# A conformer convolution's finish one attention step earlier, with two of its operations moved to VectorE

## The chip, the cores and the metric

The kernel runs on one core of one Trainium2 chip. The metric is device microseconds of one execution, given as the median of several runs. A core has TensorE (matrix products, written PE in the profile), VectorE (DVE), ScalarE (ACT), GpSimd (POOL) and SyncE (SP), each with its own queue of instructions that it takes in order; here SP issues the weight loads. All five share the on-chip memories: SBUF for tiles, and PSUM, into which TensorE writes and which VectorE and ScalarE read.

## What is computed

A trunk of two layers on 512 positions of width 1024. Each layer is a feed-forward part, a mixing part and a second feed-forward part. The change lies in the mixing part, in the convolution group:

```python
def conv_module(a, g, conv_w, conv_b, conv_norm):
    u = a * jax.nn.sigmoid(g)
    y = lax.conv_general_dilated(u, rhs, ...)      # causal, depthwise, width 31
    y = y + conv_b
    return jax.nn.silu(rms_norm(y, conv_norm))

# mixing part of a layer
a, g, q, k, v = jnp.split(rms_norm(x, mix_norm[l]) @ w_in[l], splits, axis=-1)
conv_out = conv_module(a, g, conv_w[l], conv_b[l], conv_norm[l])
# per head: two softmax maps with a relative-position bias, A1 - lambda * A2, values, RMSNorm
diff_out = diff_attention(q, k, v, rel_bias, lam, lam_init, subln_norm[l])
x = x + jnp.concatenate([conv_out, diff_out], axis=-1) @ w_out[l]
```

## The kernel before

Activations lie with features on the 128 partitions and the 512 positions along the free axis. Every large product is made of three products in a fast 32-bit format: each factor is split into a larger part (a rounded copy) and a lower part (the value minus that copy), and `mm3` adds larger x larger, larger x lower and lower x larger. For weights the larger part `whi` is made by ScalarE (L101) and the lower part `wlo` by VectorE or GpSimd (L102), from a buffer `wraw` that SP loads.

A program that schedules by estimated times places the instructions of each engine; only those wrapped in `keep_in_program_order` keep the written order. So moving one operation can change the order of its neighbours on every engine.

The mixer's stages around the change:

- `conv_in` and `project` make the convolution's inputs, queries and keys; `project_values` the values.
- `conv_taps` computes the 31 taps of four channel tiles `ys[0..3]`. Tile 0 and ten taps of tile 3 are done by ScalarE and GpSimd (L968, L969, result `yp`), the rest by VectorE (L983, result `u`). `conv_square` adds up the squares; with the last tile GpSimd multiplies all four tiles by half the gain (`ghalf`, L955).
- `rows_rstd` transposes the sum of squares on TensorE (L196), reduces it on VectorE (L200, L201) and GpSimd raises it to -1/2 (L189, `rs_y`).
- `attend(n)` runs one attention step; step n is one head of one block of 128 queries, with 512, 384, 256 and 128 keys for steps 0 to 3, 4 to 7, 8 to 11 and 12 to 15. `softmaxes` has TensorE's two scores (L1015), VectorE's pass that adds the bias and finds the minimum (L1019), ScalarE's exponential (L1023), and VectorE's reciprocal, factor and combination of the two maps (L1026, L1028, L1029). Two steps later `keys_first` transposes the map (L1036, copied by ScalarE, L1038), three steps later `values` multiplies it with the values (L1045). With a block's last head, VectorE sums squares (L1056), GpSimd makes the root, VectorE scales (L1060), and `block_out` transposes the block (L1072) and splits it into parts (L1074 ScalarE, L1075 VectorE).
- `conv_finish`, called behind one attention step, spreads the statistic over the positions (`spread`: TensorE L209, ScalarE L213) and for each of the four tiles: GpSimd multiplies by the statistic (L995), ScalarE takes the tanh (L997), VectorE forms the swish (L998), ScalarE makes the larger part (L999, into `ch`), GpSimd the lower part (L1000, into `cl`).
- `next_wo` loads and splits one of four chunks of the output weights for the convolution half; two of these calls stand behind `conv_finish`.
- The output projection (L138, L141, L142 with `ps_out`) first takes the convolution's four feature tiles for all eight output tiles, then the attention's features; VectorE adds each result to x (L1137).

PSUM has two buffers under each of the tags `sc` and `po`, which scores and output products share, two under `mm` for the value products, and one each under `tp` and `y`.

Of the kernel before, what the change touches and what calls it, by code (L numbers as in the profile page):

```python
# [14 lines left out]
AF = mybir.ActivationFunctionType  # L15
ALU = mybir.AluOpType
# [52 lines left out]
def trunk(ctx: ExitStack, tc: tile.TileContext, xt, par, lamv, relb, onehot,  # L69
          gu1, dn1, wag, wqkv, wout, gu2, dn2, out):  # L70
    nc = tc.nc
    V, S, G, T = nc.vector, nc.scalar, nc.gpsimd, nc.tensor
# [9 lines left out]
    def f32(ap):  # L82
        return ap.bitcast(F32)
# [3 lines left out]
    def bank(tag, name):  # L87
        return psum.tile([P, 512], F32, tag=tag, name=name, bufs=BANKS[tag])
# [115 lines left out]
    def spread(rc, tag, pin=False):  # L204


        ps = bank("y", "ps_spread")
        for j in range(NT):
            mm = T.transpose(ps[:, j * P : (j + 1) * P], rc[:, j : j + 1].broadcast_to([P, P]), ident)  # L209
            if pin:  # L210
                tc.keep_in_program_order(mm)
        r = act.tile([P, SEQ], F32, tag=tag, name=tag)
        S.activation(r, ps, AF.Copy)  # L213
        return r
# [585 lines left out]
    nlam, gq, gsub, ghalf = [], [], [], []  # L800
# [35 lines left out]
    def mixer(l, pr, after, turn):  # L836
        with tc.tile_pool(name="mix", bufs=1) as mp, tc.tile_pool(name="mt", bufs=2) as mt:
# [101 lines left out]
            ch, cl = acth, actl  # L939

            ys = [None] * CT
            csum = mp.tile([P, SEQ], F32, tag="csum", name="csum")

            def conv_square(c, y):
                if c == 0:
                    S.activation(csum, y, AF.Square)
                else:
                    sq = mt.tile([P, SEQ], F32, tag="csq", name="csq", bufs=1)
                    S.activation(sq, y, AF.Square)
                    G.tensor_tensor(csum, csum, sq, op=ALU.add)  # L950

                if c == CT - 1:
                    for k in range(CT):
                        tc.keep_in_program_order(
                            G.tensor_scalar(ys[k], ys[k], ghalf[l][:, k : k + 1], None, op0=ALU.mult)  # L955
                        )

            def conv_taps(c, n, then=None):

# [10 lines left out]
                if n == TAPS:  # L970
                    ys[c] = yp
                    conv_square(c, yp)
                    return
# [13 lines left out]
                if n:  # L987
                    V.tensor_tensor(ys[c], y, yp, op=ALU.add)
                conv_square(c, ys[c])

            def conv_finish(rcv):
                rcv = spread(rcv, "rb")
                for c in range(CT):
                    z = ys[c]
                    G.tensor_tensor(z, z, rcv, op=ALU.mult)  # L995
                    th = bank("y", "ps_th")
                    S.activation(th, z, AF.Tanh)  # L997
                    V.scalar_tensor_tensor(z, th, 1.0, z, op0=ALU.add, op1=ALU.mult)  # L998
                    S.activation(ch[:, c, :], z, AF.Copy)  # L999
                    G.tensor_tensor(cl[:, c, :], z, f32(ch[:, c, :]), op=ALU.subtract)  # L1000


# [76 lines left out]
            def attend(n):  # L1079
                if n < len(steps):  # L1080
                    softmaxes(*steps[n])
                if 2 <= n < len(steps) + 2:
                    keys_first(*steps[n - 2])
                if 3 <= n < len(steps) + 3:
                    values(*steps[n - 3])
                if n >= 5 and steps[n - 5][1] == HEADS - 1:
                    block_out(steps[n - 5][0])
# [23 lines left out]
            def next_wo():  # L1111
                wo.append(chunk(wout[l, 0, len(wo)], G, pin=True))
# [4 lines left out]
            next_wo()  # L1117
            for n in range(2, len(steps) + 5):
                attend(n)
                if n == 8:  # L1120
                    conv_finish(rcv)
                    next_wo()
                    next_wo()
# [3 lines left out]
            for half, t in ((0, slice(0, SEQ)), (1, slice(SEQ // 2, SEQ)), (1, slice(0, SEQ // 2))):  # L1127
                if t.stop == SEQ:
                    w = [None] * 4 if half else wo
                for m in range(KT):  # L1130
# [3 lines left out]
                    for kk in range(4):  # L1134
                        k = half * 4 + kk
# [17 lines left out]
    for l in range(DEPTH):  # L1153
        nxt = {}

        def then(l2, gain):
            def after(m):
                if m == 0:
                    nxt["p"] = Prep(l2, gain)
                nxt["p"].tile(m)  # L1160
            return after

        def last(m):
            nc.sync.dma_start(out[m], x[:, m, :])

        turn = ffn(pr, gu1[l], dn1[l], then(l, "mix_norm"), 2, *((lead, aside) if l == 0 else ()))
        mixer(l, nxt["p"], then(l, "ffn2_norm"), turn)
        ffn(nxt["p"], gu2[l], dn2[l], then(l + 1, "ffn1_norm") if l + 1 < DEPTH else last, 0)
        pr = nxt["p"]
# [74 lines left out]
```

## Time and profile before

| | us |
|---|---|
| median of 3 runs | 1775.17 (1773.5 to 1775.44) |
| the profiled execution | 1775.55 |
| its span, first to last instruction | 1773.8 |
| TensorE busy | 1762.1 |
| VectorE busy | 1420.0 |
| ScalarE busy | 995.8 |
| GpSimd busy | 999.0 |

A row of a timeline has the start in us from the span's start, the duration in us (for merged rows that of all xN together), engine, line, operation, the tile written and the tiles read, their shapes, the count, and in brackets the idle time ahead of it with the engine and line that ended it. On VectorE, ScalarE and GpSimd a row's duration runs a little past the start of the next one, so the price of an operation in a full queue is the distance of the starts. A row of a group view has the count, then total busy us and mean ns of one. A row for a tile or a line has the durations in ns as least, median and largest, and the first and the last start. In the windows the columns are the window, its length, busy us of PE, PE's weight loads, DVE, ACT and POOL with the number of instructions, the granted TensorE clock as a share of full speed, the share of the DMA engines' time and GB/s.

### The profile page before, as it was taken

What the parts mean: (1) busy time and instruction counts of PE and PEld (TensorE: products, weight loads), DVE (VectorE), ACT (ScalarE), POOL (GpSimd) and SP (SyncE); (2) the same over time, 40 slices, a digit from 0 to 9 for tenths busy, and PEclk for the clock granted to TensorE, in tenths of its full rate; (3) what the DMA queues carried; (4) which work ended last, traced back from release to release, by engine and by line L of the source; (5) the groups of instructions that cost most, each with busy time, mean ns of one, the idle gap of its engine ahead of it and who ended that gap; (6) DMA issues with size and microseconds to landing.
All of it is one profiled execution on the core that took longest, in us unless ns stands there. A gap on an engine that the chain in (4) does not pass through costs nothing.

```text
span 1773.8 us, 30569 instructions
## 1 busy us (share of the span) xinstructions
PE 1762.1 (99%) x11869; PEld 1624.1 (92%) x11869; DVE 1420.0 (80%) x2021; ACT 995.8 (56%) x1591; POOL 999.0 (56%) x665
## 2 busy tenths in 40 slices
PE   9999999999999999999999999999999999999999
PEld 7899999988788899999988999999887988999998
DVE  6988888868857878888778888877788488788885
ACT  6456566645845456556534665665558354565663
POOL 3176766379863156656304666653898432567661
PEclk9999999999999999999999999999999999999999
DMA  6233333433122233333332333334230232333332
GB/s 225 92 117 96 107 108 105 124 106 96 36 84 84 83 97 107 107 101 120 101 109 71 108 98 106 108 102 148 72 119 25 72 108 72 108 96 108 108 105 75
DMA packets 74227, 177.89 MB, mean 100 GB/s; under 512 B 8952, under 2 KB 30727, under 8 KB 74081
## 3 DMA queue, kind: packets, MB, share of 16 engines
q1 hardware_dynamic: 72480, 174.10, 31.3%
q8 instruction: 93, 1.52, 0.4%
q0 software_dynamic: 1312, 1.67, 0.3%
q14 instruction: 54, 0.43, 0.1%
q10 hardware_dynamic: 288, 0.16, 0.0%
HBM read 173.79 MB, written 3.42 MB: 100 GB/s over the span
## 4 chain that ended last, share of the span: by engine, by line
PE 89%; DVE 6%; issue 2%; POOL 2%; ACT 1%; DMA 0%; ACTq 0%; SPq 0%; DVEq 0%
PE ps_pair L378 49%; PE ps_pair L142 5%; PE ps_pair L141 5%; PE ps_pair L138 5%; DVE wlo L368 2%; PE ps_d L138 2%; PE ps_d L142 2%; PE ps_d L141 2%; PE ps_sc L1015 2%; PE ps_d L378 2%; PE ps_pair L891 2%; PE ps_pair L893 2%; PE ps_pair L892 2%; PE ps_out L138 1%; PE ps_out L141 1%
## 5 line engine op out<-in xcount | busy, mean ns | idle before, releaser
L368 DVE TENSOR_TENSOR wlo<-wraw,whi 128x1024 fp32r<-128x1024 f32 (+2 forms) x400 | 525.4, 1314 | 149.7 <-ACT whi L364 149.0
L364 ACT ACTIVATE whi<-wraw 128x1024 fp32r<-128x1024 f32 (+2 forms) x400 | 378.6, 948 | 312.1 <-PE ps_pair L378 144.5
L355 POOL TENSOR_TENSOR wraw<-wraw 128x512 f32<-128x512 f32 (+1 forms) x100 | 132.1, 1321 | 519.7 <-DVE wlo L368 316.2
L378 PE MATMUL ps_pair<-actl,whi 128*128 128x256 f32 x1088 | 307.9, 283 | 0.0
L378 PE MATMUL ps_pair<-acth,wlo 128*128 128x256 f32 x1088 | 307.9, 283 | 0.0
L378 PE MATMUL ps_pair<-acth,whi 128*128 128x256 f32 x1088 | 307.9, 283 | 0.0
L378 PE MATMUL ps_pair<-th,whi 128*128 128x256 f32 x816 | 232.5, 285 | 2.4 <-ACT keep L430 1.5
L378 PE MATMUL ps_pair<-tl,whi 128*128 128x256 f32 x816 | 230.9, 283 | 0.0
L378 PE MATMUL ps_pair<-th,wlo 128*128 128x256 f32 x816 | 230.8, 283 | 0.0
L378 PEld LDWEIGHTS ps_pair<-acth,whi 128*128 128x128 f32 x1088 | 208.9, 192 | 0.2
L378 PEld LDWEIGHTS ps_pair<-actl,whi 128*128 128x128 f32 x1088 | 208.9, 192 | 0.2
L378 PEld LDWEIGHTS ps_pair<-acth,wlo 128*128 128x128 f32 x1088 | 208.9, 192 | 0.0
L101 ACT ACTIVATE whi<-wraw 128x1024 fp32r<-128x1024 f32 (+3 forms) x124 | 122.9, 1000 | 147.9 <-PE ps_pair L141 79.7
L358 POOL TENSOR_TENSOR wraw<-wraw 128x512 f32<-128x512 f32 (+1 forms) x100 | 177.4, 1774 | 7.9
L141 PE MATMUL ps_pair<-actl,whi 128*128 128x512 f32 x448 | 174.7, 391 | 0.3
L138 PE MATMUL ps_pair<-acth,whi 128*128 128x512 f32 x448 | 173.9, 393 | 0.4 <-ACT whi L101 0.4
L142 PE MATMUL ps_pair<-acth,wlo 128*128 128x512 f32 x448 | 173.8, 390 | 0.0
L357 POOL TENSOR_TENSOR wraw<-wraw 128x512 f32<-128x512 f32 (+1 forms) x100 | 169.0, 1690 | 7.8
L356 POOL TENSOR_TENSOR wraw<-wraw 128x512 f32<-128x512 f32 (+1 forms) x100 | 166.9, 1669 | 7.6
L378 PEld LDWEIGHTS ps_pair<-th,whi 128*128 128x128 f32 x816 | 156.5, 192 | 5.3 <-ACT keep L430 4.9
L378 PEld LDWEIGHTS ps_pair<-tl,whi 128*128 128x128 f32 x816 | 156.5, 192 | 0.0
L378 PEld LDWEIGHTS ps_pair<-th,wlo 128*128 128x128 f32 x816 | 156.5, 192 | 0.0
(205 smaller groups left out, 4461.3 us busy)
## 6 DMA issues: line engine op xcount, KB each, us to landing
wraw<-in_gu SPq DMA_DIRECT2D x172, 512.0 KB, 3.5
wraw<-in_wqkv SPq DMA_DIRECT2D x24, 512.0 KB, 3.6
wraw<-in_wag SPq DMA_DIRECT2D x16, 512.0 KB, 3.6
wraw<-in_wout SPq DMA_DIRECT2D x16, 512.0 KB, 3.5
wraw<-in_dn SPq DMA_DIRECT2D x60, 128.0 KB, 3.0
wraw<-in_dn SPq DMA_DIRECT2D x20, 384.0 KB, 3.3
wraw<-in_dn SPq DMA_DIRECT2D x28, 256.0 KB, 3.3
wraw<-in_dn SPq DMA_DIRECT2D x20, 320.0 KB, 3.3
```

What stands on the lines that cost most here:

```text
L101: S.activation(hi, raw, AF.Copy)
L138: first = T.matmul(ps, wh, xh, start=start, stop=False)
L141: T.matmul(ps, wh, xl, start=False, stop=False)
L142: T.matmul(ps, wl, xh, start=False, stop=stop)
L355: G.tensor_tensor(d, g1, u1, op=ALU.add)
L356: G.tensor_tensor(u1, u1, u2, op=ALU.add)
L357: G.tensor_tensor(m0, u1, g1, op=ALU.add)
L358: G.tensor_tensor(m1, m0, g2, op=ALU.add)
L364: pinned(S.activation(hi[:, : self.cols[k]], self.raw[k][:, : self.cols[k]], AF.Copy), pin)
L368: pinned(V.tensor_tensor(out=lo[:, :c], in0=self.raw[k][:, :c], in1=f32(hi[:, :c]), op=ALU.subtract), pin)
L378: mm = T.matmul(ps, l, r, start=first and i == n == 0, stop=False, skip_group_check=True)
L891: T.matmul(ps[n], xh[:, t], wh, start=k == 0, stop=False)
```

## The change

Three edits, in both layers:

```diff
                 if c == CT - 1:
                     for k in range(CT):
-                        tc.keep_in_program_order(
-                            G.tensor_scalar(ys[k], ys[k], ghalf[l][:, k : k + 1], None, op0=ALU.mult)
-                        )
+                        V.tensor_scalar(ys[k], ys[k], ghalf[l][:, k : k + 1], None, op0=ALU.mult)
...
                     V.scalar_tensor_tensor(z, th, 1.0, z, op0=ALU.add, op1=ALU.mult)
-                    S.activation(ch[:, c, :], z, AF.Copy)
+                    V.tensor_scalar(ch[:, c, :], z, 1.0, None, op0=ALU.mult)
                     G.tensor_tensor(cl[:, c, :], z, f32(ch[:, c, :]), op=ALU.subtract)
...
             for n in range(2, len(steps) + 5):
                 attend(n)
-                if n == 8:
+                if n == 7:
                     conv_finish(rcv)
                     next_wo()
                     next_wo()
```

The four multiplications by half the gain go from GpSimd to VectorE and are no longer held in the written order; the four copies that make the larger parts go from ScalarE to VectorE; and `conv_finish` with its two `next_wo` calls is written behind step 7 where it was behind step 8. Line numbers of the changed kernel are two lower from L957 on.

## The prediction

> **What bounds the kernel now.** I read the page's engine shares first, then the windows across the first layer's mixer, then the timelines of TensorE, VectorE and GpSimd where TensorE has gaps.
>
> ```profile
> PE 1762.1 (99%) x11869; PEld 1624.1 (92%) x11869; DVE 1420.0 (80%) x2021; ACT 995.8 (56%) x1591; POOL 999.0 (56%) x665
> ```
>
> TensorE sets the time nearly everywhere, so the change can act only where TensorE waits. In the mixer of the first layer that is one place:
>
> ```profile
> 465.00:470.00 5.00, 5.00 (x22) 3.32 (x21) 2.18 (x5) 5.00 (x8) 3.97 (x4) 1.00 0.00 0
> ...
> 485.00:490.00 5.00, 5.00 (x42) 4.78 (x40) 4.31 (x21) 3.95 (x16) 3.92 (x5) 1.00 0.32 94
> 490.00:495.00 5.00, 3.20 (x20) 2.25 (x19) 4.88 (x19) 5.00 (x18) 4.67 (x6) 1.00 0.03 11
> ```
>
> ```profile
> 1370.00:1375.00 5.00, 3.20 (x20) 2.24 (x19) 4.88 (x19) 5.00 (x19) 4.68 (x6) 1.00 0.06 25
> 1375.00:1380.00 5.00, 5.00 (x25) 4.60 (x24) 3.70 (x13) 4.37 (x16) 3.29 (x4) 0.66 0.00 0
> ```
>
> The columns are window, then busy time of TensorE, its weight loads, VectorE, ScalarE and GpSimd, then the granted clock. From 490 to 495 TensorE has holes, while VectorE (4.88) and ScalarE (5.00) are full. The second layer repeats this 880 us later, and just behind its holes the granted clock is 0.66 over 5 us, so up to 5 x 0.34 = 1.7 us more are lost there. TensorE's own rows:
>
> ```profile
> 489.84 0.39 PE L1015 MATMUL ps_sc<-kt,qz 128*128 128x128 f32 x2
> 490.43 0.70 PE L1015 MATMUL ps_sc<-kt,qz 128*128 128x256 f32 x2 [0.20 <-DVE e L1029]
> 490.97 0.38 PE L1036 MATMUL ps_at<-ident,e 128*128 128x128 f32 x2
> 491.19 0.60 PE L1072 MATMUL ps_o<-ident,ov 128*128 128x128 f32 x4
> 492.05 0.49 PE L1015 MATMUL ps_sc<-kt,qz 128*128 128x128 f32 x2 [0.26 <-DVE mn L1019]
> 493.04 0.49 PE L1015 MATMUL ps_sc<-kt,qz 128*128 128x128 f32 x2 [0.50 <-DVE e L1029]
> 493.36 0.38 PE L1036 MATMUL ps_at<-ident,e 128*128 128x128 f32 x2
> 494.57 1.16 PE L1045 MATMUL ps_o<-vv,at 128*128 128x128 f32 x8 [0.83 <-DVE actl L1075]
> 495.49 0.48 PE L138 MATMUL ps_out<-acth,whi 128*128 128x512 f32 x1
> ```
>
> A 128-column piece costs 0.11 us (eight in 495.49 - 494.57 = 0.92), a 256-column score 0.22. From 489.84 to 495.49 are 5.65 us with 2x0.11 + 2x0.22 + 2x0.11 + 4x0.11 + 2x0.11 + 2x0.11 + 2x0.11 + 0.92 = 2.90 of work: **2.75 us of holes in each layer**, all released by VectorE. At 495.49 the first output product (L138) arrives and fills TensorE from there. So the question is what stands ahead of that product, and how fast VectorE gets through it:
>
> ```profile
> 481.43 0.23 DVE L201 TENSOR_SCALAR rowv<-rowv 128x4 f32<-128x4 f32 x1
> ...
> 486.04 0.62 DVE L1029 SCALAR_TENSOR_TENSOR e<-ps_sc,c,e 128x384 f32<-128x384 f32 x1
> ...
> 490.30 0.68 DVE L1060 TENSOR_TENSOR ov<-ps_o,rs_y 128x512 f32<-128x512 f32 x1
> 490.89 0.15 DVE L1026 RECIPROCAL r<-sums 128x1 f32<-128x1 f32 x1
> 491.17 0.43 DVE L1019 CUSTOM_DVE_ANT_0 ps_sc<-ps_sc,bias 128x256 f32<-128x256 f32 x1
> ...
> 491.52 0.27 DVE L1028 TENSOR_SCALAR c<-r,nlam,sums 128x1 f32<-128x1 f32 x1
> 491.70 0.28 DVE L1019 CUSTOM_DVE_ANT_0 e<-ps_sc,bias 128x128 f32<-128x128 f32 x1
> ...
> 491.91 0.68 DVE L1056 TENSOR_REDUCE so<-sq 128x4 f32<-128x512 f32 x1
> 492.51 0.47 DVE L1029 SCALAR_TENSOR_TENSOR e<-ps_sc,c,e 128x256 f32<-128x256 f32 x1
> 492.90 0.15 DVE L1026 RECIPROCAL r<-sums 128x1 f32<-128x1 f32 x1
> 492.99 0.69 DVE L998 SCALAR_TENSOR_TENSOR yp<-ps_th,yp 128x512 f32<-128x512 f32 x1
> 493.60 0.27 DVE L1028 TENSOR_SCALAR c<-r,nlam,sums 128x1 f32<-128x1 f32 x1
> 493.78 0.74 DVE L1075 SCALAR_TENSOR_TENSOR actl<-ps_o,gsub,acth 128x512 fp32r<-128x512 f32 x1
> 494.44 0.29 DVE L1019 CUSTOM_DVE_ANT_0 ps_sc<-ps_sc,bias 128x128 f32<-128x128 f32 x1
> ```
>
> Consecutive starts give VectorE's prices: L1060 0.59, L1019 0.35 (256 wide) and 0.21 (128), L1056 0.60, L1029 0.39 (256), L998 0.61, L1075 0.66, L1026 about 0.1, L1028 about 0.2. The row at 492.51 is step 10's combination; the row at 486.04 is step 7's.
>
> **The change part by part.**
>
> *Factor off GpSimd.* The rows below show the four L955 (1.57 us each) just ahead of the conv statistic's rs_y (484.02), whose input was done at 481.66 (481.43 + 0.23). Without them rs_y runs about 2.4 us earlier. What stands behind it on GpSimd stays (a 2.36 us wlo, the block's so and rs_y), so L995 starts near 481.7 + 1.0 + 2.4 + 0.2 + 1.0 = 486.3, about 3 us ahead of 489.63.
>
> ```profile
> 479.42 4.64 POOL L955 TENSOR_SCALAR u<-u,ghalf 128x512 f32<-128x512 f32 x3
> 484.02 1.03 POOL L189 TENSOR_TENSOR rs_y<-rowv,mhalf 128x4 f32<-128x4 f32 x1
> 485.03 2.36 POOL L102 TENSOR_TENSOR wlo<-wraw,whi 128x1024 fp32r<-128x1024 f32 x1
> ...
> 489.63 1.27 POOL L995 TENSOR_TENSOR yp<-yp,rb 128x512 f32<-128x512 f32 x1 [1.00 <-ACT rb L213]
> 490.86 3.20 POOL L995 TENSOR_TENSOR u<-u,rb 128x512 f32<-128x512 f32 x3
> ...
> 503.36 7.09 POOL L102 TENSOR_TENSOR wlo<-wraw,whi 128x1024 fp32r<-128x1024 f32 x3
> ```
>
> *Factor and larger parts onto VectorE.* Eight one-input SBUF operations of 128x512 per layer. The nearest rows:
>
> ```profile
> L201 DVE TENSOR_SCALAR rowv<-rowv 128x4 f32<-128x4 f32 x8 | 1.5, 182 | 0.1
> L99 DVE TENSOR_SCALAR whi<-wraw 128x128 fp32r<-128x128 f32 x1 | 0.2, 227 | 3.2 <-DMA wraw<-in_gu 3.2
> ```
>
> ```profile
> L325 DVE TENSOR_TENSOR actl<-hn,acth x32: 676/686/1786, 60.8 to 1490.2; 128x512 fp32r<-128x512 f32 x32
> ```
>
> ```profile
> L999 ACT ACTIVATE acth<-u x6: 622/632/652, 496.0 to 1382.2; 128x512 fp32r<-128x512 f32 x6
> ```
>
> From 4 to 128 elements the price grows by 45 ns, 0.36 ns an element; 384 more make 0.227 + 0.14 = 0.37, my lower end and, being the same kind of operation, the value I take rounded to 0.4. The upper end is the largest L325 of the same size, 1.8. Three of the four factors stand ahead of step 2's passes, where the window 465 to 470 has VectorE idle for 2.8 us: they cost nothing, and were that cover gone, 1.2 us. The fourth and the four parts fall into the full stretch. ScalarE gets 4 x 0.63 = 2.5 us back, but it does not release TensorE here.
>
> *Finish one step earlier.* The built order tells what that moves. TensorE's queue is in order, and the first output product stands no earlier in it: the same scores, plus two more value products of step 10 (4 x 0.11) and one more block transpose (4 x 0.11), so 0.88 us more work stands ahead, and the product now waits for step 10's combination and its copy. On VectorE the finish used to stand behind that combination (L998 first at 492.99, after 492.51). Now three L998, two parts, one L1075 and a second L1060 stand ahead of it. The two wout loads keep their place in SP's queue, and their GpSimd halves (503.36) still follow the last lower part, early enough for a product some 30 matmuls behind the first. The new order also adds a wait: ScalarE's first tanh (L997) now stands ahead of step 9's second exponential, and VectorE's factor for step 9 queues behind that; L995 ends near 486.3 + 1.3 = 487.6, about when ScalarE gets there, so I cost it at nothing, and at what L995 is late otherwise.
>
> *The sum.* From step 7's combination to the start of step 10's: before, 492.51 - 486.04 = 6.47 us, waits included. After, VectorE's queue holds between them: the combination itself 0.57, six passes of 256 (2.1), two of 128 (0.42), two combinations (0.8), reciprocals and factors (1.15), two L1060 (1.2), one L1056 (0.6), one L1075 (0.66), three L998 (1.83), two parts (0.8): 10.1 us. Step 7's combination itself starts some 0.3 earlier, at 485.7 (two passes of 256 have moved behind it, the fourth factor ahead of it). Step 10's ends at 485.7 + 10.1 + 0.4 = 496.2; transposes 0.22, ScalarE's copy
>
> ```profile
> 495.56 0.42 ACT L1038 ACTIVATE at<-ps_at 128x256 f32<-128x256 f32 x1
> ```
>
> of 0.42, value products 0.44 and about 0.1 for each of four hand-overs make 1.5: the first product starts near 497.7. By before's pace with 0.88 us more work it would be 495.49 + 0.88 = 496.4. That is +1.3 us a layer. In its fullest neighbourhood VectorE still idled 0.69 us in 485 to 490; I add half a microsecond for such hand-overs, which my sum lacks: **+1.8 us a layer, +3.6 in all**, with a low end of +1.0 a layer (no hand-overs, copies at 0.37 in part hidden) and a high end of +3.2 (each of the two parts ahead at about 1.1, halfway to the stretched row). Behind that product I find nothing new late: the parts for its later steps are done before TensorE reaches them. The profiled execution is 1775.55 us (span 1773.8 and 1.75 around it), 0.4 over the median of the three runs, so 1775.55 + 3.6 = **1779.2**.
>
> **The rivals.**
>
> *A. The holes close.* If the finish, 3 us earlier, let TensorE fill its holes, 2 x 2.75 = 5.5 us would go, and with them the clock loss of up to 1.7: 1768.4 to 1770. For it: VectorE releases every hole, and GpSimd and ScalarE get lighter. Against: no product moved ahead in TensorE's queue, and VectorE, which is full, got more. It decides only if step 10's combination comes before about 494.
>
> *B. Slower by less than can be told.* The low end, or the clock loss of the second layer falling away: 1775.55 + 3.6 - 1.7 = 1777.5. For it: the clock fell in one layer only, although both have the same holes, so whether it falls is close to a toss. [...]
>
> *C. VectorE and GpSimd shut each other out.* L325 takes 0.68 at best and 1.79 at worst. In the finish GpSimd is nearly always busy (4.67 of 5), with operations of 1.1 to 2.4 us; if each part waited for the rest of one, some 0.6 to 1.1, two of them ahead would add 1.2 to 2.2 a layer: 1779.2 + 3 = 1782. [...] No row here has a one-input VectorE operation of this size under a busy GpSimd.
>
> **How the numbers follow.** Forecast 0.46, A 0.10, B 0.30, C 0.14. About 0.2%, 3.6 us, is what can be told from no change. Slower by more than that: forecast and C, 0.60; within: B, 0.30; faster: A, 0.10. The range for 8 in 10 leaves out A and the far end of C: 1775.5 to 1783.0.
>
> **What would show it.** Right: TensorE's first L138 on ps_out some 2 us later in the first layer (near 497.7), more than 3.5 us of holes ahead of it; step 10's combination ending near 496; L995's first start near 486.5; VectorE's copies near 0.4 us. Wrong: TensorE's holes under 2 us, or the first product before 496; or copies of 0.6 us and more (then C); or a stall behind the first product, which I do not expect.

## The result, and the profile after

| | before | after |
|---|---|---|
| median, us | 1774.98 | 1777.11 |
| lowest to highest (22 runs each) | 1773.31 to 1775.80 | 1776.32 to 1779.22 |
| span of the profiled execution | 1773.8 | 1775.2 |

The ratio is 1.0015, with a 95% interval of 1.0009 to 1.0021: the changed kernel is slower by 2.1 us as the medians have it (2.7 by the ratio), where 3.6 were forecast and 1779.2 as the time.

From the page of the changed kernel, the engine shares, then from its windows the stretch of the first layer in question and the one of the second layer where the clock had fallen before (columns as above):

```profile
PE 1760.0 (99%) x11869; PEld 1621.4 (91%) x11869; DVE 1431.9 (81%) x2037; ACT 992.3 (56%) x1583; POOL 987.0 (56%) x657
```

```profile
485.00:490.00 5.00, 5.00 (x40) 4.58 (x40) 4.89 (x20) 4.59 (x15) 4.92 (x7) 1.00 0.31 105
490.00:495.00 5.00, 2.89 (x19) 2.17 (x17) 5.00 (x19) 4.34 (x15) 4.60 (x6) 1.00 0.02 3
495.00:500.00 5.00, 3.79 (x21) 3.13 (x22) 4.68 (x17) 2.40 (x7) 2.76 (x4) 1.00 0.00 0
1375.00:1380.00 5.00, 3.08 (x20) 2.56 (x21) 5.00 (x19) 3.89 (x13) 3.09 (x3) 1.00 0.00 0
```

VectorE is now full for the whole of 490 to 495, ScalarE no longer is (5.00 before, 4.34 now), and TensorE's holes reach on into 495 to 500. The granted clock is 1.00 in all four windows. TensorE's timeline in the first layer:

```profile
489.98 0.38 PE L1034 MATMUL ps_at<-ident,e 128*128 128x128 f32 x2
491.67 0.71 PE L1043 MATMUL ps_o<-vv,at 128*128 128x128 f32 x4 [1.31 <-ACT at L1036]
492.22 0.60 PE L1013 MATMUL ps_sc<-kt,qz 128*128 128x256 f32 x2
...
493.51 0.71 PE L1043 MATMUL ps_o<-vv,at 128*128 128x128 f32 x4 [0.25 <-ACT at L1036]
494.06 0.39 PE L1013 MATMUL ps_sc<-kt,qz 128*128 128x128 f32 x2
495.66 0.66 PE L1070 MATMUL ps_o<-ident,ov 128*128 128x128 f32 x4 [1.22 <-DVE ov L1058]
...
497.37 0.71 PE L1043 MATMUL ps_o<-vv,at 128*128 128x128 f32 x4 [0.55 <-ACT at L1036]
497.84 0.47 PE L138 MATMUL ps_out<-acth,whi 128*128 128x512 f32 x1
```

The first output product starts at 497.84, 2.35 us later than before (495.49). The holes have split in two groups, one ahead of 491.67 and one ahead of 495.66. At the prediction's prices they are 4.3 us from 489.98 on (7.86 us with 3.5 of work). VectorE's timeline over the same stretch, from step 7's combination to step 10's and the part behind it, with no idle time in front of any row:

```profile
485.54 0.62 DVE L1027 SCALAR_TENSOR_TENSOR e<-ps_sc,c,e 128x384 f32<-128x384 f32 x1
...
488.82 0.68 DVE L996 SCALAR_TENSOR_TENSOR yp<-ps_th,yp 128x512 f32<-128x512 f32 x1
489.42 0.15 DVE L1024 RECIPROCAL r<-sums 128x1 f32<-128x1 f32 x1
489.53 0.77 DVE L997 TENSOR_SCALAR acth<-yp 128x512 fp32r<-128x512 f32 x1
490.22 0.26 DVE L1026 TENSOR_SCALAR c<-r,nlam,sums 128x1 f32<-128x1 f32 x1
...
493.81 0.42 DVE L997 TENSOR_SCALAR acth<-u 128x512 fp32r<-128x512 f32 x1
494.15 0.26 DVE L1026 TENSOR_SCALAR c<-r,nlam,sums 128x1 f32<-128x1 f32 x1
494.34 0.67 DVE L996 SCALAR_TENSOR_TENSOR u<-ps_th,u 128x512 f32<-128x512 f32 x1
494.94 0.67 DVE L1058 TENSOR_TENSOR ov<-ps_o,rs_y 128x512 f32<-128x512 f32 x1
495.53 0.14 DVE L1024 RECIPROCAL r<-sums 128x1 f32<-128x1 f32 x1
495.60 0.46 DVE L1027 SCALAR_TENSOR_TENSOR e<-ps_sc,c,e 128x256 f32<-128x256 f32 x1
495.99 0.41 DVE L997 TENSOR_SCALAR acth<-u 128x512 fp32r<-128x512 f32 x1
```

The way from 485.54 to 495.60 is 10.06 us of work; before it was 6.47. I call it the walk below. GpSimd's timeline shows what the factor's leaving did there:

```profile
482.08 1.02 POOL L189 TENSOR_TENSOR rs_y<-rowv,mhalf 128x4 f32<-128x4 f32 x1 [4.27 <-DVE rowv L201]
```

```profile
486.65 1.27 POOL L993 TENSOR_TENSOR yp<-yp,rb 128x512 f32<-128x512 f32 x1
```

`rs_y` starts 1.94 us earlier than before (484.02), the finish 3 us earlier (489.63), and TensorE nevertheless comes later to the output products.

### The profile page after: what moved, and what is told of

It is laid out like the page before. It is cut to its first block, busy times and chain, and to the rows that moved or that the text cites. A ratio compares the mean times of both kernels' runs of the same rounds, so it can differ in the third digit from the quotient of the medians.

```text
span 1775.2 us, 30569 instructions
## 1 busy us (share of the span) xinstructions
PE 1760.0 (99%) x11869; PEld 1621.4 (91%) x11869; DVE 1431.9 (81%) x2037; ACT 992.3 (56%) x1583; POOL 987.0 (56%) x657
## 4 chain that ended last, share of the span: by engine, by line
PE 87%; DVE 8%; issue 2%; POOL 2%; ACT 1%; DMA 0%; ACTq 0%; SPq 0%; DVEq 0%
PE ps_pair L378 49%; PE ps_pair L142 5%; PE ps_pair L141 5%; PE ps_pair L138 5%; DVE wlo L368 2%; PE ps_d L138 2%; PE ps_d L142 2%; PE ps_d L141 2%; PE ps_d L378 2%; PE ps_pair L892 2%; PE ps_pair L893 2%; PE ps_pair L891 2%; PE ps_out L142 1%; PE ps_out L138 1%; PE ps_out L141 1%
## 5 line engine op out<-in xcount | busy, mean ns | idle before, releaser
L355 POOL TENSOR_TENSOR wraw<-wraw 128x512 f32<-128x512 f32 (+1 forms) x100 | 131.7, 1317 | 520.8 <-DVE wlo L368 332.4
L358 POOL TENSOR_TENSOR wraw<-wraw 128x512 f32<-128x512 f32 (+1 forms) x100 | 177.3, 1773 | 7.8
L356 POOL TENSOR_TENSOR wraw<-wraw 128x512 f32<-128x512 f32 (+1 forms) x100 | 164.9, 1649 | 7.6
```

Source lines behind the costliest of these rows:

```text
L355: G.tensor_tensor(d, g1, u1, op=ALU.add)
L356: G.tensor_tensor(u1, u1, u2, op=ALU.add)
L358: G.tensor_tensor(m1, m0, g2, op=ALU.add)
```

## The experiments

Each experiment was timed in five rounds beside the kernel before. The table has what was read from each: the walk (start of step 7's combination to start of step 10's on VectorE, first layer, profiled execution), the start of the first output product there, the median, the ratio to before with its interval, and the runs whose granted clock was 1.000 over the whole span, with their median. The last two columns are needed because one stretch of 3.41 us at half the granted clock, as in the profiled execution of before, loses half of it, 1.7 us, and lowers the mean clock of the run to 0.999, and because kernels differ in how often they have one. The clock is given to three places, so a run listed at 0.999 need not have had such a stretch: of before's 63 runs below 1.000, ten took 1773.4 to 1774.2, as long as the runs at 1.000, and 53 took 1774.8 or more (median 1775.4, 1.6 above the 1773.8 of the runs at 1.000).

| kernel | walk | product | median | ratio [95%] | runs at full clock | their median |
|---|---|---|---|---|---|---|
| before (96 runs beside the experiments) | 6.47 | 495.49 | 1774.3 to 1775.0 | | 33 of 96 | 1773.8 |
| the change | 10.06 | 497.84 | 1777.11 | 1.0015 [1.0009, 1.0021] | 18 of 22 | 1776.97 |
| finish behind step 7 only | 6.47 | 496.82 | 1775.02 | 1.0001 [0.9992, 1.0010] | 5 of 11 | 1773.91 |
| factor and parts, step 8 | 10.08 | 497.69 | 1777.03 | 1.0015 [1.0006, 1.0024] | 8 of 11 | 1776.93 |
| factor only | 8.27 | 496.33 | 1773.86 | 0.9996 [0.9987, 1.0005] | 10 of 11 | 1773.88 |
| parts only | 6.47 | 495.81 | 1775.10 | 1.0001 [0.9992, 1.0009] | 2 of 11 | 1773.45 |
| change, parts of tiles 2 and 3 only | 8.28 | 496.37 | 1773.87 | 0.9994 [0.9985, 1.0003] | 10 of 11 | 1773.86 |
| change, parts of tiles 0 and 1 only | 10.07 | 499.17 | 1777.25 | 1.0017 [1.0008, 1.0025] | 4 of 11 | 1777.03 |
| change, parts in a longer form | 10.60 | 497.98 | 1779.88 | 1.0028 [1.0018, 1.0038] | 2 of 8 | 1778.05 |
| change, block scaling by ScalarE | 10.42 | 498.17 | 1778.16 | 1.0019 [1.0011, 1.0028] | 5 of 11 | 1777.06 |
| factor only, block scaling by ScalarE | 9.31 | 496.36 | 1775.31 | 1.0002 [0.9993, 1.0011] | 10 of 11 | 1775.32 |
| factor by ScalarE | 6.52 | 495.24 | 1774.08 | 0.9996 [0.9988, 1.0005] | 7 of 11 | 1774.14 |
| factor by VectorE, 9 taps | 7.66 | 496.71 | 1775.24 | 1.0003 [0.9994, 1.0012] | 10 of 11 | 1775.14 |
| factor by ScalarE, 9 taps | 7.34 | 496.34 | 1775.78 | 1.0006 [0.9997, 1.0015] | 10 of 11 | 1775.76 |

A start is counted from the first instruction of its own execution, and executions are not aligned: with the same order of instructions up to there, step 7's combination starts at 486.04 (before), 486.56 (finish behind step 7 only) and 485.55 (parts only). The column of the product carries this half microsecond; the walk does not (6.47 in all three).

### Which of the three edits

The first two runs separate the place of the finish from the rest.

```diff
-                if n == 8:
+                if n == 7:
```

> Only the finish written behind step 7; factor on GpSimd and larger parts on ScalarE as before. Theory (VectorE's queue ahead of step 10's combination decides, and that queue is made by the operations, not by the place in the text): the built order of every engine is the same as before, so 1775.0 +-0.5, ratio 1.000, first output product at 495.5 in the first layer. Rival (the move behind step 7 itself brings the new order and the loss, as my prediction wrote it): a ratio of 1.0005 or more, first output product at 496.4 or later.

The second has the other two edits and leaves the place at step 8:

```diff
-                        tc.keep_in_program_order(
-                            G.tensor_scalar(ys[k], ys[k], ghalf[l][:, k : k + 1], None, op0=ALU.mult)
-                        )
+                        V.tensor_scalar(ys[k], ys[k], ghalf[l][:, k : k + 1], None, op0=ALU.mult)
...
-                    S.activation(ch[:, c, :], z, AF.Copy)
+                    V.tensor_scalar(ch[:, c, :], z, 1.0, None, op0=ALU.mult)
```

> Factor and larger parts by VectorE, the finish still behind step 8. Theory: the built order of every engine is the same as in the changed kernel, so 1777.1 +-0.5, ratio 1.001 to 1.0015, first output product at 497.8. Rival (the move behind step 7 is part of the loss): between 1775 and 1776.5.

Both came out as the theory had it: 1775.02 and 1777.03. The built order of the instructions on each of the five engines is the same for step 7 as for step 8, with the other two edits and without them. The scheduler places the finish by its estimated times, so writing it one step earlier does nothing at all. One reading does not fit the expectation, a first product at 496.82 instead of 495.5. Of the 1.33 us, 0.52 is that the whole stretch lies later in that execution (step 7's combination at 486.56 for 486.04). The rest falls where the clock did: from 495.03 it was at half speed, just when the last value products ahead of the product ran. From the windows of this kernel (finish behind step 7 only):

```profile
495.03:498.44 3.41, 3.35 (x14) 3.25 (x15) 2.12 (x11) 2.59 (x8) 3.29 (x3) 0.50 0.02 5
```

The other two take the factor alone (first half of the diff above) and the parts alone (second half).

> Only the factor by VectorE; finish behind step 8, parts by ScalarE. Theory (queue walk): between step 7's combination (start near 485.5) and step 10's there are 7.97 us of VectorE work (two swishes, one L1075, one L1060, no parts), so step 10's ends near 494.0 and the first output product, which here stands behind its transposes, starts near 494.5 with 1.0 us more attention work done ahead of it: 1.5 to 2 us less of holes a layer, 1771 to 1773, ratio 0.998. Rival C (GpSimd and VectorE shut each other out, and that is the loss): the factor operations at 0.7 us and more, and slower than before, 1776 or more. Rival (all hidden): 1775 +-0.5.

> Only the larger parts by VectorE; finish behind step 8, factor on GpSimd. Theory: up to step 10's combination VectorE's queue is that of before (the parts stand behind it, since the finish still waits for GpSimd until 489.6); the first part stands behind one L1075 and one pass, ends near 495.2, and the first output product starts at 495.5 to 495.9: 1774.5 to 1776, ratio 0.9998 to 1.0006. Rival (each part on VectorE costs, wherever it stands): 1776 to 1777 with copies of 0.7 us and more.

The parts alone: 1775.10, as the theory had it. The factor alone: 1773.86, neither the 1771 to 1773 of the theory nor the 1776 of rival C. Its timelines of VectorE (steps 7, 10 and 11) and TensorE show which step of that expectation was wrong:

```profile
485.36 0.62 DVE L1027 SCALAR_TENSOR_TENSOR e<-ps_sc,c,e 128x384 f32<-128x384 f32 x1
...
493.63 0.47 DVE L1027 SCALAR_TENSOR_TENSOR e<-ps_sc,c,e 128x256 f32<-128x256 f32 x1
...
494.79 0.47 DVE L1027 SCALAR_TENSOR_TENSOR e<-ps_sc,c,e 128x256 f32<-128x256 f32 x1
```

```profile
496.16 0.38 PE L1034 MATMUL ps_at<-ident,e 128*128 128x128 f32 x2
496.33 0.50 PE L138 MATMUL ps_out<-acth,whi 128*128 128x512 f32 x1
```

Step 10's combination is where I put it (493.63 + 0.39 for 494.0), but the transposes right ahead of the product (496.16) are those of step 11, whose combination ends at 495.2; I had taken them for step 10's. So one more step is done ahead of the product, the product comes 0.84 us later, and in all TensorE gains nothing: at full clock 1773.88, against 1773.8 before.

The four runs make a square. At full clock, before, the factor alone and the parts alone (only two such runs) are within 0.5 us of each other, and both together are 3.1 us slower. Each of the two edits by itself costs nothing: with the factor on GpSimd the finish starts too late for its work to get ahead of step 10's combination, and without the parts on VectorE what gets ahead is short enough.

### Which of the parts

If it is what stands ahead of step 10's combination that costs, the four parts must not be equal: two stand ahead, two behind. Two mirror images of the changed kernel, one with ScalarE for tiles 0 and 1, one with ScalarE for tiles 2 and 3:

```diff
-                    V.tensor_scalar(ch[:, c, :], z, 1.0, None, op0=ALU.mult)
+                    if c < 2:
+                        S.activation(ch[:, c, :], z, AF.Copy)
+                    else:
+                        V.tensor_scalar(ch[:, c, :], z, 1.0, None, op0=ALU.mult)
```

> The changed kernel, but the larger parts of tiles 0 and 1 by ScalarE as before; those of tiles 2 and 3 stay on VectorE. Theory (only what stands on VectorE ahead of step 10's combination costs): VectorE's queue up to there is that of the factor alone (7.97 us), so step 10's combination starts at 493.6, the first output product at 496.3 with the same work ahead, and the time is that of the factor alone: 1773.9 +-0.6, no clock loss. Rival (each of the parts costs its 0.4 us wherever it stands): halfway, 1775.4 +-0.4.

The mirror image has `c >= 2` in place of `c < 2`.

> The mirror image: larger parts of tiles 0 and 1 by VectorE, those of tiles 2 and 3 by ScalarE as before. Theory: the walk up to step 10's combination is that of the changed kernel (10.0 us, two parts, three swishes, two L1058), so the combination starts at 495.5, the first output product at or behind 497.7, and the whole loss is there: 1776.4 to 1777.6. Rival (each part costs wherever it stands): 1775.4 +-0.4.

1773.87 and 1777.25: the parts of tiles 0 and 1 bring the whole loss, those of tiles 2 and 3 none. In TensorE's timeline of the kernel that has only the late parts on VectorE, and then of the one that has only the early ones:

```profile
494.96 0.66 PE L1073 MATMUL ps_o<-ident,ov 128*128 128x128 f32 x4
...
496.37 0.50 PE L138 MATMUL ps_out<-acth,whi 128*128 128x512 f32 x1
```

```profile
495.97 0.66 PE L1073 MATMUL ps_o<-ident,ov 128*128 128x128 f32 x4 [1.23 <-DVE ov L1061]
...
499.17 0.78 PE L138 MATMUL ps_out<-acth,whi 128*128 128x512 f32 x1
```

With the early parts the block's transposes wait 1.23 us for VectorE, as in the changed kernel (1.22); with the late ones they wait for nothing. (499.17 stands behind step 11's transposes, and the clock of that execution fell at 497.97.) The two parts are not the whole of the 1.8 us by which the walks differ: with them on VectorE the built order also puts a third swish (0.60) and a second block scaling (0.59) ahead of step 10's combination. Which part of the loss is the copies' own and which is that order was not taken apart.

### A longer part

The parts by an operation of VectorE that takes longer, as a test of the dose and of rival C:

```diff
-                    V.tensor_scalar(ch[:, c, :], z, 1.0, None, op0=ALU.mult)
+                    V.scalar_tensor_tensor(ch[:, c, :], z, 0.0, z, op0=ALU.mult, op1=ALU.add)
```

> The changed kernel with its four larger parts made by a two-input operation of VectorE (z times 0 plus z) in place of the one-input copy. Theory (VectorE's queue decides, C adds a few tenths): each costs about 0.61 us like the other two-input rows, none is stretched under a busy GpSimd; two ahead make +0.4, the stretch of 0.36 that the first copy showed is gone, so step 10's combination starts at 495.6 to 495.9 and the time stays 1776.8 to 1777.6. Rival C (the loss comes from copies that wait for GpSimd): 1775.5 or less.

VectorE's timeline of this kernel:

```profile
489.05 1.05 DVE L997 SCALAR_TENSOR_TENSOR acth<-yp 128x512 fp32r<-128x512 f32 x1
...
493.61 0.68 DVE L997 SCALAR_TENSOR_TENSOR acth<-u 128x512 fp32r<-128x512 f32 x1
```

The stretch of the first part is still there (1.05 against 0.68), so the walk grew by 0.54 and did not stay as it was, and the time grew with it: at full clock 1778.05 (two runs only) for 1776.97, which is 0.54 a layer. My expectation missed by that stretch and by the clock, which fell in 6 of 8 runs. The dose fits the theory; that a gain would come from another form, as C would have it, does not.

### Work for other engines

Two kernels hand VectorE's block scaling to ScalarE, one from the changed kernel and one from the factor alone:

```diff
-                V.tensor_tensor(
-                    ov, po.rearrange("p (h d) -> p h d", h=HEADS),
-                    ro.unsqueeze(2).broadcast_to([P, HEADS, VD]), op=ALU.mult,
-                )
+                for g in range(HEADS):
+                    S.activation(ov[:, g, :], po[:, g * VD : (g + 1) * VD], AF.Copy, scale=ro[:, g : g + 1])
```

> The changed kernel with the block's scaling (L1058) by ScalarE in four pieces instead of VectorE, 2 x 0.6 us less on VectorE ahead of step 10's combination in place of two reciprocal-sized rows. Theory: the walk is 9.0 us, that combination starts at 494.6, the first output product near 496.8 with 0.3 us more done ahead of it: 1.3 us a layer back, 1774.4 +-0.7. Rival (ScalarE, which gets about 1.2 us a block, becomes the late one; or VectorE's queue isn't what is late): 1776 or more.

> Factor by VectorE, larger parts by ScalarE, and the block's scaling (L1058) by ScalarE in four pieces. Theory: the walk is 7.4 us, step 10's combination starts near 492.9, the first output product stands right behind its transposes (the order shows 8 pieces fewer ahead than with the factor alone) and starts near 494.0: 1.5 us a layer less than before, 1770.5 to 1772, faster than both kernels, no clock loss. Rival (ScalarE, full here, is late with exponentials and parts): 1774 or more.

Both missed on the side of the rival: 1778.16 (at full clock 1777.06, as the changed kernel) and 1775.31. In the second, ScalarE's timeline has the four pieces, and VectorE's waits right behind them:

```profile
486.66 1.14 ACT L1059 ACTIVATE ov<-ps_o,rs_y 128x128 f32<-128x128 f32 x4
```

```profile
488.29 0.16 DVE L1024 RECIPROCAL r<-sums 128x1 f32<-128x1 f32 x1 [0.33 <-ACT ps_sc L1021]
...
489.61 0.16 DVE L1024 RECIPROCAL r<-sums 128x1 f32<-128x1 f32 x1 [0.33 <-ACT ps_sc L1021]
```

The pieces take 1.0 us of ScalarE for 0.6 us of VectorE, ScalarE's exponentials come later, and VectorE now waits for them: the walk is 9.31 us, of which VectorE's rows fill 7.99, where 7.4 was forecast for the whole. The first kernel has the same two waits (at 488.21 and 489.54). In these kernels ScalarE bounds the stretch as well as VectorE.

Three more looked for a version faster than both. The factor by ScalarE; 9 taps for 10 in tile 3's share of ScalarE and GpSimd, so that the statistic comes earlier; and both.

```diff
+                        S.activation(ys[k], ys[k], AF.Copy, scale=ghalf[l][:, k : k + 1])
...
-POOL_TAPS = (TAPS, 0, 0, 10)
+POOL_TAPS = (TAPS, 0, 0, 9)
```

> Factor by ScalarE in place of GpSimd or VectorE (scaled copies, about 0.6 us each), parts by ScalarE, finish behind step 8. Theory: VectorE loses nothing to the factor, and by the built order only 6.0 us stand on it between step 7's combination (start near 485.3) and step 10's, two swishes and one L1075 among them; step 10's starts at 491.5 to 493, and the first output product, which stands where it stood before, starts at 493 to 494: 1.5 to 2.5 us a layer less than before, 1769 to 1771.5, no clock loss. Rival (ScalarE is as full as VectorE, so what is laid on it comes back as waits for exponentials, as with the block's scaling): 1774 or more.

> Factor by VectorE, and tile 3's convolution with 9 taps by ScalarE and GpSimd for 10, so that the statistic comes about 1.5 us earlier. Theory: one tap more (0.66 us) on VectorE lies in its idle time of 465 to 470; the walk to step 10's combination is 7.5 us with three swishes in it, the combination starts near 493.2, the first output product near 494.5 with 0.7 us more done ahead than before: 1.2 to 1.7 us a layer less, 1770.5 to 1772. Rival (the tap delays VectorE's attention steps as much as it speeds up the finish): 1773.5 to 1775.

> Factor by ScalarE, and 9 taps for 10. Theory: the walk is 7.1 us with three swishes and no L1075 in it, step 10's combination starts at 492.5 to 493.5, the first output product (same place as before in TensorE's queue) at 493.3 to 494.3: 1.2 to 2.2 us a layer less than before, 1769.5 to 1771.5. Rival (ScalarE late): 1774 or more.

All three missed: 1774.08, 1775.24 and 1775.78, where 1769 to 1772 was forecast. None is faster than before by more than its interval (the factor by VectorE alone, with the parts of tiles 2 and 3 or without, comes nearest: its median is 1.1 us lower because it keeps the full clock). With the factor by ScalarE step 10's combination starts at 492.46, as forecast, but the product only at 495.24, since other work is late in its place, as TensorE's timeline shows:

```profile
494.14 0.49 PE L1013 MATMUL ps_sc<-kt,qz 128*128 128x128 f32 x2 [0.65 <-DVE mn L1017]
...
495.24 0.50 PE L138 MATMUL ps_out<-acth,whi 128*128 128x512 f32 x1
```

Here a score waits for VectorE's pass (L1017). So the walk decides only while it is the longest chain; in the kernels with 8.3 us and less something else holds the product, such as this pass or step 11's transposes with the factor alone. With 9 taps the product comes at 496.71 and 496.34; which chain holds it there was not followed further.

## Why the prediction was right, and where it was wrong

**The walk: right.** Step 7's combination was forecast at 485.7 and came at 485.54; the work between it and step 10's at 10.1, measured 10.06; its end at 496.2, measured 495.60 + 0.39 = 496.0; the first product at 497.7, measured 497.84. L995 (now L993) was forecast to start at 486.3 and started at 486.65. That the starts agree to 0.2 us is in part luck, since those of one order differ by half a microsecond between executions. The closeness of the walk's sum is luck too: the two parts ahead took 0.69 and 0.34 us from start to start where 0.4 each was put, and the other rows together came out 0.3 lower. The 0.1 us for each of four hand-overs behind that combination was the author's estimate, and no run shows it; the rows have 497.84 - 495.99 = 1.85 us for the stretch that was put at 1.5, with a score ahead of the transposes in it (496.16 to 496.44). No stall came up behind the product.

**Slower, but by less: the terms mis-sized.** By the prediction's own division the result is not its forecast (0.46) but rival B (0.30): 2.1 us is under the 3.6 it set as told from no change, and 1777.11 lies at B's 1777.5. (With 22 runs each, the interval does tell 2.1 us from nothing.) Two terms make the difference of 2.1 us between 1779.2 and 1777.11. The half microsecond a layer for hand-overs was not there in that size: 497.84 - 495.49 less 0.88 of work done ahead is 1.47 a layer (the two executions are nearly aligned: ahead of the stretch a score's row starts at 467.79 before and at 467.71 after), and the runs at full clock say (1776.97 - 1773.8) / 2 = 1.59, against 1.8 forecast; that is 0.4 us of the 2.1. The rest is the clock. The forecast added 3.6 to one execution that had had a stretch of 3.41 us at half clock, and so held the loss for granted. Of the 96 runs of before 63 were below full clock (53 of them also longer); of the change's 22 only 4 were, and these took 1778.5 to 1779.2, where the forecast was. Rival B named this term, and it decided the size. B took whether the clock falls for a toss; the last section has what the traces show of it.

**Finish one step earlier: wrong cause.** The prediction told the new order of the engines' queues as the effect of the move behind step 7. The order was read rightly, but the move has no part in it (same built order, 1775.02 with the move alone). It comes from the factor and the parts together.

**ScalarE "does not release TensorE here": wrong for after.** For before, the rows name VectorE for 1.79 of the 2.75 us of holes and nothing for the rest, so "all released by VectorE" was more than they show. In the changed kernel three of the four holes shown end with ScalarE's copy of the transposed map. From its ScalarE timeline, ahead of the largest:

```profile
489.56 0.69 ACT L1072 ACTIVATE acth<-ps_o,gsub 128x512 fp32r<-128x512 f32 x1
490.12 0.61 ACT L1052 ACTIVATE sq<-ps_o 128x512 f32<-128x512 f32 x1
490.60 0.23 ACT L1050 ACTIVATE se<-sums 128x4 f32<-128x4 f32 x1
490.70 0.62 ACT L995 ACTIVATE ps_th<-u 128x512 f32<-128x512 f32 x1
491.22 0.40 ACT L1036 ACTIVATE at<-ps_at 128x256 f32<-128x256 f32 x1
```

The transposes started at 489.98 and the copy at 491.22, behind four operations queued on ScalarE. It did not spoil the sum, whose end came where VectorE's walk put it, but two later expectations that gave ScalarE more work went wrong on the same belief.

**Rival A** fell: holes did not close. **Rival C**: the stretched rows are there, and their price is small. The factor's six rows on `u`, then one of its two on `yp` with GpSimd's operation beside it:

```profile
L954 DVE TENSOR_SCALAR u<-u,ghalf x6: 737/896/1636, 409.7 to 1358.8; 128x512 f32<-128x512 f32 x6
```

```profile
459.10 1.07 DVE L954 TENSOR_SCALAR yp<-yp,ghalf 128x512 f32<-128x512 f32 x1
```

```profile
458.59 1.29 POOL L950 TENSOR_TENSOR csum<-csum,csq 128x512 f32<-128x512 f32 x1 [0.59 <-ACT csum L946]
...
496.47 1.09 POOL L998 TENSOR_TENSOR actl<-u,acth 128x512 fp32r<-128x512 f32 x1 [1.07 <-DVE acth L997]
```

GpSimd's ends at 458.59 + 1.29 = 459.88, and VectorE's 0.29 us later, at 459.10 + 1.07 = 460.17; the same form takes 0.41 while GpSimd is idle (L997 at 495.99, in GpSimd's 1.07 us of waiting ahead of 496.47). So the factor's price was wrong (0.74 to 1.64 us for the 0.4 forecast) and its cover held: the factor alone costs nothing. In the stretch that matters only the first of the two parts was stretched, by 0.36 us.

## What to carry to other kernels

Before costing a move in a program whose order a scheduler makes, compare the built orders with each edit alone: an edit that moves nothing is worth nothing, and the order may come from another one. Where several engines are full at once, as here, the operations that cost were those ahead of a release on their own queue (parts of tiles 0 and 1), and those behind it cost nothing (tiles 2 and 3); count exactly that stretch, and find by its tile which step a waiting instruction belongs to. A sum made against one profiled execution must say whether the clock fell in that execution (here to half for 3.41 us), and runs are compared at the same granted clock.

## What the hardware showed that was not expected

In four profiled executions the clock fell behind a stretch in which TensorE still worked. Windows of 3.41 us, ahead of the loss and at it, in before and then in the kernel with the parts only; the third is a stretch of the changed kernel:

```profile
1371.62:1375.03 3.41, 1.82 (x12) 1.16 (x10) 3.41 (x16) 3.41 (x11) 3.09 (x5) 1.00 0.00 0
1375.03:1378.44 3.41, 3.41 (x17) 3.31 (x17) 2.41 (x10) 2.80 (x11) 2.86 (x3) 0.50 0.00 0
```

```profile
490.64:494.05 3.41, 1.85 (x13) 1.19 (x10) 3.37 (x12) 3.31 (x11) 3.09 (x4) 1.00 0.00 0
494.05:497.46 3.41, 3.37 (x15) 3.28 (x16) 2.21 (x11) 1.72 (x6) 2.24 (x2) 0.50 0.02 5
```

```profile
494.20:497.61 3.41, 1.64 (x13) 1.18 (x12) 3.41 (x14) 2.34 (x8) 2.25 (x3) 1.00 0.02 5
```

Each of the four losses lasts 3.41 us at half clock and follows 3.41 us in which TensorE's rows fill 1.6 to 1.9 us (1.82, 1.85, 1.89 with the finish behind step 7 only, 1.63 with the early parts only). So low a filling is not enough by itself: in the changed kernel's stretch they fill 1.64, and the clock stayed.

Where the stretch begins may matter too. The clock record of before's trace starts at 6.28, at full clock, and falls to half at 1375.03 and once more behind the last instruction, at 1774.39; that of the changed kernel starts at 4.90 and falls only behind the last instruction, at 1776.42 (the two falls at the end stand behind 3.41 us without a row of TensorE). To the nanosecond these falls come 1368.745, 1768.104 and 1771.518 us behind the start of their record. Divided by 401, 518 and 519 each gives 3.4133 us, and the loss at 1375.03 lasts 3.413: in these two traces the falls lie on equal steps of the loss's own length. Counted on these steps, the holes of before's first layer left 2.00 us of rows in a step (490.98 to 494.39) and the clock stayed; those of the second layer, which lie otherwise against the steps, left 1.82, and it fell. On the changed kernel's steps the least of the first layer is 1.94 (493.00 to 496.41). How far a step must empty is not placed by these runs: one with 1.70 kept the clock (the changed kernel, 1769.59 to 1773.00).

The kernel before has its holes close together; the change splits them, has more of them, and loses the clock less often. That the split does this is not shown: kernels with holes much like the change's were below full clock in 6 of 8 runs (longer form) and 7 of 11 (early parts).

VectorE's operation with two SBUF inputs is stretched beside GpSimd too: in the kernel with the longer form the part on `yp`, whose place in the changed kernel lies beside GpSimd's multiplications (L993, 1.09 and 1.27 us), took 1.05 us, the others 0.68 (both inputs are the same tile). In before, seven of the 32 rows of L325 took 1.78 to 1.79 us, all of them beside GpSimd's L356 to L358 (1.62 to 2.16 us); the least of the 32 is 0.68. One row of GpSimd's L355, which began at 940.92, took 5.18 us for a median of 1.29; the five rows of L325 from 940.85 to 944.62 took 0.70 each.
